# The pool of the weights placed behind the pools of the split inputs and the norm tiles

## The chip, the cores and the metric

The kernel runs on one core of one Trainium2 chip. The metric is the device time of one execution in microseconds (us); of several executions the median is given. A difference under about 0.2% of this kernel's time (2.5 us) can't be told from none.

## The reference

A decoder trunk of two layers over 512 tokens of width 1024, all in float32:

```
layer 0:  x = x + s5_mixer(rms_norm(x))       # state-space mixer, GELU, then z = y @ w_glu, gated
          x = x + conv_ffn(rms_norm(x))
          k, v = split(rms_norm(x) @ kv_w)    # shared keys and values
layer 1:  x = x + attention(rms_norm(x) @ w_q, k, v) @ w_o    # 16 heads of 64, stick-breaking, causal
          x = x + conv_ffn(rms_norm(x))
out = rms_norm(x)

conv_ffn(h):  g, u = split(h @ w_up)          # 2 x 2816 columns
              return (silu(conv3(g)) * u) @ w_down
```

## The kernel before

All activations lie transposed in SBUF: 128 channels on the partitions, 512 tokens along the free dimension, so that `x` is 8 tiles of 128x512. Each large product is float32 split in two: an operand is taken apart into a high part (`h`, rounded to float32r) and the rest (`l`), and the product is high x high + high x low + low x high. The helper `gemm` does this for one block of weights:

```
def gemm(bank, w, xs, k0=0, k1=KT, first=None, last=None):
    hi, lo = w
    for k in range(k0, min(k1, len(xs))):
        xh, xl = xs[k]
        c = slice(k * P, (k + 1) * P)
        mm(bank, hi[:, c], xh, ...)
        mm(bank, hi[:, c], xl, ...)
        mm(bank, lo[:, c], xh, ...)
```

In each `mm` (line 106) the second argument is loaded into TensorE as weights (a PEld row of the profile, 128x128, that is 512 bytes of each partition), and the third is streamed through (a PE row, 128x512, that is 2048 bytes of each partition). In these rows the weights' tile ends in `h` or `l` after the name of the matrix. The stages, with the tiles that meet in them (`out<-streamed, weights`; the profile prints the two operands in alphabetical order):

- State-space mixer, 0 to about 224 us. Its output product is `gl<-yh,wvh`, `gl<-yl,wvh`, `gl<-yh,wvl`.
- Feed-forward of layer 0, about 224 to 592 us, in three chunks of 8, 7 and 7 blocks of the 22 hidden blocks. Up-projections `fg` and `fu` stream the split input (`xh`, `xl`, or both halves of `xhl`) past `wgh`/`wgl` and `wuh`/`wul`; the down-projection `fd` streams the hidden activations `ah`, `al` past `wdh`/`wdl`.
- Attention, about 592 to 858 us. `kqb` (keys and queries) streams `xh`, `xl`, `xhl` past `awh`/`awl`; `v` (values) does it the other way round: the weights `awh`/`awl` are streamed, 256 columns at a time, and `xh`, `xl`, `xhl` are loaded. `z` and `ob<-wh,vv` are the attention's inner products, among tiles of the attention's own pools; `ob<-oh,awh` and its like are the output projection.
- Feed-forward of layer 1 with the final norm, about 858 us to the end. Its last block of `fd` is computed in two halves of 256 tokens.

Each weight block comes by DMA into a `raw` tile, ScalarE makes `hi` of it and VectorE `lo`. The order of the instructions is written out by hand in the mixer and in attention and left to the framework's scheduler elsewhere.

SBUF is given out by pools, which lie one behind the other in the order in which they are opened, and a tile keeps its place for the whole run. The ones concerned:

- `const`: parameters, `x`, constants.
- `wp`: 9 tiles of 4096 bytes per partition: three buffers each of `raw`, `hi` and `lo` (the mixer's first product and its rotation table use the same buffers).
- `tp`: 10 tiles of 2048 bytes (tag `ta`) and 3 of 4096 bytes (tag `tb`); `split_x` puts the split inputs `xh`, `xl`, `xhl` there, and the mixer its `u`, `u8`, `cm`.
- `sm`: 3 tiles of 2048 bytes for the norms and 18 tiny tiles of 32 bytes, 6720 bytes in all.
- the work pool of the current stage (`s5t`, `ff0`, `att`, `ff1`, and the pools nested in it): `yh`, `yl`, `ah`, `al`, `oh`, `ol`, `lh`, `wh`, `vv` and the rest.

All tiles of `wp`, `tp` and the work pools that TensorE's long products use are multiples of 512 bytes long, and the weights' slices are 512 bytes apart. So where an operand starts, counted modulo 512 bytes, depends on its pool alone.

Of the kernel before, what the change touches and what calls it, by code (L numbers as in the profile page):

```python
# [47 lines left out]
def trunk(ctx: ExitStack, tc: tile.TileContext, A, out):  # L48
# [1 line left out]
    V, SC, PE, GP = nc.vector, nc.scalar, nc.tensor, nc.gpsimd  # L50

    const = ctx.enter_context(tc.tile_pool(name="const", bufs=1))
    wp = ctx.enter_context(tc.tile_pool(name="wp", bufs=3))
    tp = ctx.enter_context(tc.tile_pool(name="tp", bufs=1))
    sm = ctx.enter_context(tc.tile_pool(name="sm", bufs=2))
    dr = ctx.enter_context(tc.tile_pool(name="dr", bufs=3, space=DRAM))

    cur = {}
# [1432 lines left out]
```

## Time and profile before

| | |
|---|---|
| median of 3 executions | 1237.41 us (1237.14 to 1238.03) |
| the profiled execution | 1236.96 us, of which the span from first to last instruction is 1235.2 us |
| granted TensorE clock | 0.997 |
| PE busy | 1207.6 us (98%), 6411 matrix products |
| DVE, ACT, POOL busy | 809.6, 539.3, 24.2 us |
| chain of waits that ended last | PE 89%, DVE 8% |

Times in the profile are counted from the span's start. PE is TensorE streaming, PEld its weight load, DVE is VectorE, ACT ScalarE, POOL GpSimd, SP the queue that issues most DMAs. The duration of a matrix product in a row holds the pipeline's depth as well; what a product costs in a dense row of them is the distance from one start to the next.

### The profile page before, as it was taken

What the parts mean: (1) busy time and instruction counts of PE and PEld (TensorE: products, weight loads), DVE (VectorE), ACT (ScalarE), POOL (GpSimd) and SP (SyncE); (2) the same over time, 40 slices, a digit from 0 to 9 for tenths busy, and PEclk for the clock granted to TensorE, in tenths of its full rate; (3) what the DMA queues carried; (4) which work ended last, traced back from release to release, by engine and by line L of the source; (5) the groups of instructions that cost most, each with busy time, mean ns of one, the idle gap of its engine ahead of it and who ended that gap; (6) DMA issues with size and microseconds to landing.
All of it is one profiled execution on the core that took longest, in us unless ns stands there. A gap on an engine that the chain in (4) does not pass through costs nothing.

```text
span 1235.2 us, 16227 instructions
## 1 busy us (share of the span) xinstructions
PE 1207.6 (98%) x6411; PEld 982.8 (80%) x6411; DVE 809.6 (66%) x1284; ACT 539.3 (44%) x866; POOL 24.2 (2%) x65
## 2 busy tenths in 40 slices
PE   7989999999999999999999999999999999999995
PEld 3457788788888888888889898888888888888884
DVE  7999764665435635557878989878655346536554
ACT  5234453433223323334577878765433233323331
POOL 1011020000000000000000000000000000000000
PEclk9999999999999999999999999999999999999998
DMA  5565443233233233233211211123233232332322
GB/s 199 150 166 140 122 124 98 86 102 98 90 102 99 82 106 101 92 91 100 76 51 53 82 55 48 39 86 103 86 102 97 91 103 86 91 113 88 94 75 69
DMA packets 55068, 118.47 MB, mean 96 GB/s; under 512 B 12912, under 2 KB 28528, under 8 KB 54992
## 3 DMA queue, kind: packets, MB, share of 16 engines
q1 hardware_dynamic: 50880, 105.55, 27.9%
q0 software_dynamic: 3248, 11.54, 3.1%
q8 instruction: 50, 0.82, 0.3%
q10 hardware_dynamic: 864, 0.35, 0.1%
q14 instruction: 26, 0.21, 0.1%
HBM read 109.03 MB, written 8.39 MB: 95 GB/s over the span
## 4 chain that ended last, share of the span: by engine, by line
PE 89%; DVE 8%; ACT 1%; issue 1%; DMA 1%; SPq 0%; DVEq 0%; ACTq 0%
PE fd L106 20%; PE fu L106 19%; PE fg L106 19%; PE kqb L106 7%; PE gl L106 6%; PE z L106 5%; PE ob L106 5%; PE v L106 4%; DVE k L112 2%; DVE p L112 1%; PE u L106 1%; PE y L106 1%; DVE cm L112 1%; DVE u L112 1%; DVE rv L670 1%
## 5 line engine op out<-in xcount | busy, mean ns | idle before, releaser
L106 PE MATMUL fd<-ah,wdh 128*128 128x512 f32 (+1 forms) x359 | 140.5, 391 | 0.0
L106 PE MATMUL fd<-ah,wdl 128*128 128x512 f32 (+1 forms) x359 | 139.2, 388 | 0.0
L106 PE MATMUL fd<-al,wdh 128*128 128x512 f32 (+1 forms) x359 | 137.9, 384 | 0.0
L112 DVE TENSOR_TENSOR x<-x,fd 128x512 f32<-128x512 f32 (+1 forms) x49 | 33.1, 676 | 119.8 <-PE fd L106 119.8
L157 ACT CAST wuh<-wur 128x1024 fp32r<-128x1024 f32 x44 | 46.4, 1054 | 134.4 <-PE fg L106 118.0
L157 ACT CAST wdh<-wdr 128x896 fp32r<-128x896 f32 (+1 forms) x48 | 47.1, 982 | 128.0 <-PE fd L106 98.2
L112 DVE TENSOR_TENSOR g<-fg,rb 128x512 f32<-128x512 f32 x44 | 30.4, 691 | 96.3 <-PE fg L106 93.5
L106 PE MATMUL fu<-xh,wuh 128*128 128x512 f32 x220 | 86.0, 391 | 0.0
L106 PE MATMUL fg<-xh,wgl 128*128 128x512 f32 x220 | 85.8, 390 | 0.0
L106 PE MATMUL fg<-xh,wgh 128*128 128x512 f32 x220 | 85.7, 390 | 0.0
L106 PE MATMUL fg<-xl,wgh 128*128 128x512 f32 x220 | 85.6, 389 | 0.0
L106 PE MATMUL fu<-xh,wul 128*128 128x512 f32 x220 | 85.6, 389 | 0.0
L106 PE MATMUL fu<-xl,wuh 128*128 128x512 f32 x220 | 85.6, 389 | 0.0
L112 DVE TENSOR_TENSOR u<-fu,rb 128x512 f32<-128x512 f32 x44 | 30.4, 691 | 80.5 <-PE fu L106 80.5
L106 PE MATMUL fu<-xhl,wuh 128*128 128x512 f32 x264 | 81.8, 391 | 0.0
L106 PE MATMUL fg<-xhl,wgh 128*128 128x512 f32 x264 | 81.5, 389 | 0.0
L106 PEld LDWEIGHTS fd<-ah,wdl 128*128 128x128 f32 x359 | 67.4, 188 | 15.2
L106 PEld LDWEIGHTS fd<-al,wdh 128*128 128x128 f32 x359 | 67.4, 188 | 14.8 <-issue 0.2
L106 PEld LDWEIGHTS fd<-ah,wdh 128*128 128x128 f32 x359 | 67.5, 188 | 13.2 <-issue 0.2
L157 ACT CAST wgh<-wgr 128x1024 fp32r<-128x1024 f32 x44 | 46.3, 1053 | 71.0 <-PE fd L106 33.0
L106 PE MATMUL u<-xg,wi 128*128 128x512 f32 x128 | 63.5, 628 | 7.5 <-ACT xg L270 7.5
L109 DVE SCALAR_TENSOR_TENSOR acc<-g,cw,acc 128x511 f32<-128x511 f32 x88 | 65.8, 747 | 2.4 <-ACT acc L832 0.9
(247 smaller groups left out, 2799.1 us busy)
## 6 DMA issues: line engine op xcount, KB each, us to landing
wgr<-in_w_up SPq DMA_DIRECT2D x44, 512.0 KB, 3.5
wur<-in_w_up SPq DMA_DIRECT2D x44, 512.0 KB, 3.5
wdr<-in_w_dn SPq DMA_DIRECT2D x32, 448.0 KB, 3.3
wdr<-in_w_dn SPq DMA_DIRECT2D x16, 512.0 KB, 3.5
wvr<-in_w_glu POOLq DMA_DIRECT2D x12, 512.0 KB, 3.8
ks<-kx SPq DMA_DIRECT2D x32, 128.0 KB, 2.5
m<-ks SPq DMA_DIRECT2D x8, 512.0 KB, 4.1
awr<-in_w_k SPq DMA_DIRECT2D x8, 512.0 KB, 3.5
```

Source lines behind the costliest of these rows:

```text
L106: PE.matmul(o, lhsT=lhsT, rhs=rhs, start=start, stop=stop, skip_group_check=True)
L109: (eng or V).scalar_tensor_tensor(out=o, in0=a, scalar=s, in1=b, op0=op0, op1=op1)
L112: (eng or V).tensor_tensor(out=o, in0=a, in1=b, op=op)
L157: SC.copy(out=hi, in_=raw)
L670: V.tensor_tensor_scan(out=rv[:, c], data0=decay[n], data1=wv[:, c], initial=0.0, op0=MUL, op1=ADD)
```

## The change

```
-    wp = ctx.enter_context(tc.tile_pool(name="wp", bufs=3))
     tp = ctx.enter_context(tc.tile_pool(name="tp", bufs=1))
     sm = ctx.enter_context(tc.tile_pool(name="sm", bufs=2))
+    wp = ctx.enter_context(tc.tile_pool(name="wp", bufs=3))
     dr = ctx.enter_context(tc.tile_pool(name="dr", bufs=3, space=DRAM))
```

Every engine has the same instructions in the same order with the same waits. Only the places in SBUF differ (bytes from the start of a partition, and the remainder modulo 512):

| pool | before | modulo 512 | after | modulo 512 |
|---|---|---|---|---|
| `wp` (36864 bytes) | 34976 | 160 | 74464 | 224 |
| `tp` (32768 bytes) | 71840 | 160 | 34976 | 160 |
| `sm` (6720 bytes) | 104608 | 160 | 67744 | 160 |
| work pools | 111328 | 224 | 111328 | 224 |

The 6720 bytes of `sm` are 13 times 512 and 64 more, which is why what lies behind `sm` starts at another remainder than what lies ahead of it.

More of the change, by code (lines that the diff above doesn't have):

```diff
@@ L52, in trunk @@
     const = ctx.enter_context(tc.tile_pool(name="const", bufs=1))
-    wp = ctx.enter_context(tc.tile_pool(name="wp", bufs=3))
     tp = ctx.enter_context(tc.tile_pool(name="tp", bufs=1))
     sm = ctx.enter_context(tc.tile_pool(name="sm", bufs=2))
+    wp = ctx.enter_context(tc.tile_pool(name="wp", bufs=3))
     dr = ctx.enter_context(tc.tile_pool(name="dr", bufs=3, space=DRAM))
```

## The prediction

> **What bounds the kernel now.** I read the totals and the chain of waits of the page first, then busy time by stage, then who waits for whom on TensorE.
>
> ```profile
> PE 1207.6 (98%) x6411; PEld 982.8 (80%) x6411; DVE 809.6 (66%) x1284; ACT 539.3 (44%) x866; POOL 24.2 (2%) x65
> PE 89%; DVE 8%; ACT 1%; issue 1%; DMA 1%; SPq 0%; DVEq 0%; ACTq 0%
> ```
> ```profile
> 0.00:157.00 157.00, 142.46 (x1340) 90.04 (x1341) 138.16 (x326) 66.09 (x151) 18.61 (x55) 1.00 0.53 153
> 157.00:224.00 67.00, 67.00 (x294) 54.77 (x293) 38.47 (x42) 27.47 (x36) 5.61 (x11) 1.00 0.38 116
> 224.00:614.00 390.00, 389.44 (x1763) 322.10 (x1762) 224.24 (x303) 140.30 (x178) 0.00 (x0) 1.00 0.31 95
> 614.00:858.00 244.00, 244.00 (x1400) 215.28 (x1400) 206.81 (x344) 183.69 (x355) 0.00 (x0) 1.00 0.20 61
> 858.00:1235.00 377.00, 364.65 (x1622) 300.59 (x1620) 201.93 (x271) 121.79 (x148) 0.00 (x0) 0.99 0.30 92
> ```
> ```profile
> PE stat L106 <- DVE acc L112: 0.5, 1, 0.5
> ```
>
> The windows' columns are PE, PEld, DVE, ACT and POOL busy (instructions), granted clock, DMA share, GB/s. From 157 us on TensorE is busy without a break; the last row is everything it waited for from 224 to 1220 us: 0.5 us. Nothing there can be won or lost by a DMA, by VectorE or by ScalarE as long as they keep this far ahead. Only the first 157 us hang on VectorE as well (138.16 busy). So the change acts on the time through one thing above all: how far apart TensorE's products follow each other. That is the view to read closely, and it shows something odd.
>
> ```profile
> L106 PE MATMUL fg<-xh,wgh x35: 389/389/390, 870.9 to 938.9; 128*128 128x512 f32 x35
> L106 PE MATMUL fd<-ah,wdh x59: 394/394/395, 949.8 to 989.6; 128*128 128x512 f32 x59
> L106 PE MATMUL fd<-al,wdh x59: 387/388/389, 950.0 to 989.8; 128*128 128x512 f32 x59
> L106 PE MATMUL fd<-ah,wdl x58: 392/392/393, 950.2 to 989.4; 128*128 128x512 f32 x58
> L106 PE MATMUL gl<-yh,wvh x91: 388/388/389, 162.1 to 223.9; 128*128 128x512 f32 x91
> L106 PE MATMUL ob<-oh,awh x34: 397/397/398, 834.2 to 857.3; 128*128 128x512 f32 x34
> ```
> ```profile
> 314.59 43.96 PE fd L106 x192
> 601.08 5.75 PE v L106 x48
> 826.88 31.26 PE ob L106 x137
> 947.18 43.96 PE fd L106 x192
> 1067.35 38.47 PE fd L106 x168
> ```
>
> Upper fence: one product's own rows (duration min/median/max, first and last start). Lower fence: stretches of the chain (start, length, count). From start to start:
> - `fg`, `fu`: between the first and the last of the 35 lie six rounds of 48 products (24 `fg`, 24 `fu`) and 12 more of the last `fg`: 300 in 68.0 us, 226.7 ns each.
> - `fd`: 192 in 43.96 us, 229.0 ns, twice over, and 168 in 38.47 us, 229.0. Within a group of three the durations are always 394, 388, 392.
> - `gl`: 90 groups of three in 61.8 us, 228.9 ns.
> - `ob` at the end of attention: 33 groups of three in 23.1 us, 233.3 ns.
>
> Same instruction, same shape, same clock, nothing waited for; and min, median and max differ by 2 ns, so this isn't disturbance by other engines. What differs is where the operands lie. `fg` streams from `tp` (160 modulo 512) past weights of `wp` (160): offset 0. `fd`, `gl` and `ob` stream from a work pool (224) past weights at 160: offset +64 bytes. I take it that TensorE's streaming and its load of the next weights meet in SBUF, and that the offset between the two, modulo some period, decides how often.
>
> That it is the offset and not the place of the streamed tile alone is shown by 256-column products. `v` (160 past 160) stands above, 48 in 5.75 us: 119.8 ns. The halved `fd` at the end (224 past 160) starts 20 products in 2.36 us, 118.0 ns:
>
> ```profile
> 1215.53 0.28 PE L106 MATMUL fd<-ah,wdh 128*128 128x256 f32 x1
> ...
> 1217.89 0.28 PE L106 MATMUL fd<-ah,wdl 128*128 128x256 f32 x1
> ```
>
> Here offset +64 is the better one, so 224 is no bad place in itself.
>
> **The change part by part.** Nothing is added, removed or reordered on any engine or queue. Three kinds of pairs change their offset.
>
> 1. `fd`, `gl`, `ob`: +64 becomes 0, the offset of `fg`. Price: 226.7 each.
>  - `fd`: 345 full-width products of each of three kinds, 1035 x (229.0 - 226.7) = 2.4 us less.
>  - `gl`: its last 300 or so lie in the PE-bound part, x 2.2 = 0.7 less; the rest lie beside VectorE's work before 157 us and count nothing.
>  - `ob`: 192; some 102 of them at 233.3, x 6.6 = 0.7, and 90 at about 229, x 2.3 = 0.2: 0.9 less.
> 2. `v` (streams weights past split inputs): 0 becomes +64. 384 products of 256 columns x (118.0 - 119.8) = 0.7 less. The 42 half-width `fd` go the other way: 0.1 more.
> 3. `fg`, `fu` and `kqb`: 0 becomes -64, which no row of before has. That is 44 x 48 = 2112 and 16 x 24 = 384 products, 2496 in all, two thirds of the long ones. Bounds: the best that an offset did is the 1.8 ns won at 256 columns, the worst the 6.6 ns of `ob`: from -4.5 to +16.5 us. I take 0.
>
> Why 0: the steps have a size. 256 more columns cost 226.7 - 119.8 = 106.9 ns, 0.418 per column; the 6.6 ns between `ob` and `fg` are 16 columns, 64 bytes. `fd` loses one such step in three products (3 x 2.3 = 6.9). And a row of products at offset 0 needs time to settle after other work:
>
> ```profile
> 740.21 0.40 PE L106 MATMUL kqb<-xl,awh 128*128 128x512 f32 x1
> ...
> 742.74 0.39 PE L106 MATMUL kqb<-xh,awh 128*128 128x512 f32 x1
> ...
> 745.23 0.39 PE L106 MATMUL kqb<-xh,awl 128*128 128x512 f32 x1
> ```
>
> The 11 products to 742.74 take 230 ns each, the 11 after it 226.4. So about 37 ns, five to six steps of 6.6, are lost before the row finds its place, then none. Two streams that repeat every 128 bytes would be in step after one lost step; five or six fit a period of 512 bytes, in which -64 and +64 are different cases. If slipping later mends every phase at offset 0, and +64 is just over the edge (one step in three), then -64 lies on the other side of offset 0, away from that edge. That is a guess from few rows, and its chance is put accordingly.
>
> The Trainium skill (TensorE: Matmul & The Clock Gate, "Step-by-step: what each phase is for") says that TensorE has two independent SBUF read ports, so that loading the next weights takes no bandwidth from the running product. By that rule the pools' order would not matter at all; the trace's 226.7 against 229.0 and 233.3 disagrees unless something else than the offset makes them.
>
> Other engines: `hi` and `lo` are made from `raw` inside `wp`, so their mutual offsets stay; the mixer's rotation table meets other tiles from `wp` in ten steps before 157 us. No row prices that; DVE's 138 us of work there would have to change by 2% to show. DMAs land in `raw` at another place with the same length.
>
> Sum: -2.4 - 0.7 - 0.9 - 0.7 + 0.1 = -4.6 us, plus 2496 x 0. Against the profiled execution's 1236.96 us that is 1232.4; the median stands 0.45 above that execution, so 1232.8.
>
> **The rivals.**
> - *-64 costs what +64 costs* (2.3 ns): 2496 x 2.3 = 5.7 more, sum +1.1, 1238.5 us: no change. For it: symmetry, and a period of 128 bytes, in which they are the same offset. Against: the five to six steps above.
> - *-64 settles like `ob`, one step in every product*: 16.5 more, sum +11.9, 1249.3 us, slower by 1%. It decides alone from 2.8 ns per product on, since 2496 x 2.8 covers the 4.6 won and 2.5 more. For it: the same offset +64 is seen in two states, 229.0 and 233.3. Against: of some 1600 long products at +64 only the 100 or so of late `ob` stayed in the bad one.
> - *-64 is better than 0*, as +64 is at 256 columns: up to 4.5 less, 1228.3 us. Against: at 512 columns no steady row is under 226.7.
> - *The offset doesn't matter* and the work pool's tiles are slow for a reason that stays: 1237.4 us, the median of before. Against: the 256-column rows. The Trainium skill's rule of two read ports (above) would give this too.
>
> **How the numbers follow.** Chances: 0.40 for my sum, 0.27 for the mirror image, 0.18 for a dear -64 (half or all of the products in the bad state), 0.09 for a better -64, 0.06 for no effect. The range reaches from 1227.5 (a better -64) to 1241 (past the mirror image's 1238.5, with a few products in the bad state); it leaves out nearly all of the dear case. The likeliest case's own range is 1231 to 1234.5. Faster by over 0.2% (2.5 us, which a measurement can tell): my sum and the better case, 0.48. Slower: the dear case and a little of the mirror image, 0.22. The rest, 0.30, is the same.
>
> **What would show it.** Right: the chain's `fd` x192 in 43.5 us instead of 43.96, with durations 389 throughout; `gl` and late `ob` at 226.7; `v` x48 at 5.66. The disputed term is read from `fg<-xh,wgh` x35 between its first and last start: 68.0 us if -64 costs nothing, 68.7 in the mirror image, 70.0 if dear. The prediction is wrong if `fg` and `fu` lose more than 1 ns each, or if `fd` stays at 229.0.

## The result, and the profile after

The changed kernel takes 1247.4 us at the median (1246.99 to 1248.08) against 1237.04 us (1236.81 to 1238.03): ratio 1.0081, 95% interval 1.0071 to 1.0092. It is slower by 10 us, where 4.6 us less was forecast; the case that came true is the second rival, a dear -64. The profiled execution took 1247.35 us, its span 1245.5.

The totals, the share of the chain of waits, and everything TensorE waited for from 224 to 1230 us, show the same machine as before, PE-bound, with no new wait:

```profile
PE 1217.5 (98%) x6411; PEld 981.2 (79%) x6411; DVE 809.2 (65%) x1284; ACT 539.8 (43%) x866; POOL 24.3 (2%) x65
PE 89%; DVE 8%; DMA 1%; ACT 1%; issue 1%; SPq 0%; DVEq 0%; ACTq 0%
```
```profile
PE stat L106 <- DVE acc L112: 0.3, 1, 0.3
```

PE is busy for 9.9 us more, the span is 10.3 longer, and the other engines' sums are what they were (DVE 809.6, now 809.2). So the products themselves follow each other more slowly. The same products as in the prediction (duration min/median/max, first and last start):

```profile
L106 PE MATMUL fg<-xh,wgh x35: 393/393/398, 875.7 to 945.7; 128*128 128x512 f32 x35
L106 PE MATMUL fd<-ah,wdh x64: 389/389/398, 954.1 to 997.0; 128*128 128x512 f32 x64
L106 PE MATMUL fd<-al,wdh x64: 389/389/395, 954.4 to 997.2; 128*128 128x512 f32 x64
L106 PE MATMUL fd<-ah,wdl x64: 389/389/393, 954.6 to 997.4; 128*128 128x512 f32 x64
L106 PE MATMUL gl<-yh,wvh x92: 389/389/389, 161.9 to 223.8; 128*128 128x512 f32 x92
L106 PE MATMUL ob<-oh,awh x35: 389/389/389, 837.6 to 862.0; 128*128 128x512 f32 x35
```

`fg` needs 70.0 us for its 300 products, 233.3 ns each: the value that the prediction named for a dear -64. `fd` has the flat 389 that `fg` had. `gl` starts 273 products (three for each of 91 steps) in 61.9 us, 226.7 ns each, and late `ob` has 389 where it had 397.

The chain of waits, as far as it answers to the stretches shown of before (start, length, count), with one more row of before behind it:

```profile
155.46 68.97 PE gl L106 x303
316.72 43.54 PE fd L106 x192
438.66 38.10 PE fd L106 x168
606.48 5.65 PE v L106 x48
689.38 5.60 PE kqb L106 x24
832.34 30.54 PE ob L106 x137
954.28 43.54 PE fd L106 x192
```
```profile
434.76 38.47 PE fd L106 x168
```

`fd` x192 fell from 43.96 to 43.54, `v` x48 from 5.75 to 5.65, `ob` x137 from 31.26 to 30.54, `gl` from 69.57 to 68.97. What lies between two stretches of `fd` is a chunk's up-projection: from 314.59 + 43.96 to 434.76 us it took 76.2 us before; from 316.72 + 43.54 to 438.66 it takes 78.4. Added up over the run, by the first starts of each stage in the two traces: six up-projections +13.4 us, six down-projections -2.3, attention -0.6, mixer -0.1; together +10.4 us, which is the longer span (10.3 from the rounded spans). `gl` won 0.60 us, but in the changed kernel its stretch begins 0.49 later, so the mixer's end gains almost nothing; why its first part ends later isn't known.

### The profile page after: what moved, and what is told of

It is laid out like the page before. It is cut to its first block, busy times and chain, and to the rows that moved or that the text cites. A ratio compares the mean times of both kernels' runs of the same rounds, so it can differ in the third digit from the quotient of the medians.

```text
span 1245.5 us, 16227 instructions
## 1 busy us (share of the span) xinstructions
PE 1217.5 (98%) x6411; PEld 981.2 (79%) x6411; DVE 809.2 (65%) x1284; ACT 539.8 (43%) x866; POOL 24.3 (2%) x65
## 4 chain that ended last, share of the span: by engine, by line
PE 89%; DVE 8%; DMA 1%; ACT 1%; issue 1%; SPq 0%; DVEq 0%; ACTq 0%
PE fu L106 20%; PE fg L106 19%; PE fd L106 19%; PE kqb L106 7%; PE gl L106 6%; PE z L106 5%; PE ob L106 5%; PE v L106 4%; DVE k L112 2%; DVE p L112 1%; PE u L106 1%; PE y L106 1%; DVE cm L112 1%; DVE u L112 1%; DVE rv L670 1%
## 5 line engine op out<-in xcount | busy, mean ns | idle before, releaser
L106 PEld LDWEIGHTS fd<-ah,wdh 128*128 128x128 f32 x359 | 67.4, 188 | 13.9 <-issue 0.2
L106 PEld LDWEIGHTS fd<-ah,wdl 128*128 128x128 f32 x359 | 67.4, 188 | 13.4
```

The costliest lines, as they stand in the source:

```text
L106: PE.matmul(o, lhsT=lhsT, rhs=rhs, start=start, stop=stop, skip_group_check=True)
```

## The experiments

Theory: the spacing of TensorE's long products is set by the offset between the streamed tile and the weights, modulo some number of bytes. Rivals: it is the place itself (how far back the weights lie, which pools are neighbours), or each tile's own remainder. The runs move pools alone; the instructions stay, but for the last one's mixer.

**All offsets 0, in either order (e1_all0, e2_all0_behind).** The tiny tiles of `rstd` get a pool of their own, `ti`, ahead of everything:

```
+    ti = ctx.enter_context(tc.tile_pool(name="ti", bufs=2))   # e1: ti, wp, tp, sm
     ...                                                       # e2: ti, tp, sm, wp
-        v = sm.tile([P, 4], F32, name="sv")                   # and six like it
+        v = ti.tile([P, 4], F32, name="sv")
```

e1_all0:

> The 18 tiny tiles (576 bytes) lie in a pool of their own ahead of the weights' pool, in the order of before, so that weights, split inputs and work pools all start at 224 modulo 512: every long product has offset 0. Theory offset (the offset of streamed tile and weights modulo 512 sets the spacing): fg, fu, fd, gl, late ob all at 226.7 ns, v of 256 columns at 119.8; the time is 3.9 us under before, 1233.2 us (ratio 0.9968). Rival place (weights that start at 224 modulo 512, or that lie farther back, are loaded later in each product): fg and fu at 233.3 as in the changed kernel, time near 1247 us.

e2_all0_behind:

> The same with the order of the changed kernel: tiny tiles first, then split inputs, norms, weights, work pools; all start at 224 modulo 512 and the weights' pool lies at the very same bytes as in the changed kernel. Theory offset: as the run before, 1233.2 us, fg at 226.7. Rival place: the weights haven't moved against the changed kernel, so fg and fu stay at 233.3, time near 1247 us.

Measured: 1232.92 us, ratio to before 0.9962 (0.995 to 0.9975), and 1233.68 us, 0.9964 (0.9951 to 0.9976). First e1, then e2:

```profile
L106 PE MATMUL fg<-xh,wgh x35: 389/389/389, 868.1 to 936.1; 128*128 128x512 f32 x35
```
```profile
944.41 43.52 PE fd L106 x192
```
```profile
L106 PE MATMUL fg<-xh,wgh x35: 389/389/389, 868.8 to 936.8; 128*128 128x512 f32 x35
```

`fg` needs 68.0 us again, 226.7 ns each, and now `fd` does too. In e2 the weights lie at the very bytes where they lie in the changed kernel; only the split inputs (by 576 bytes), the norms and the tiny tiles moved, and the whole loss is gone. So it isn't the place of the weights. Both kernels beat before and after; the 0.8 us between the two can't be told from none.

**Same offsets, other places (e3_place).** Pools in the order `tp`, `ti`, `wp`, `sm`:

> Split inputs, tiny tiles, weights, norms, work pools: the weights lie directly behind the split inputs and 6 KB nearer to them than in the changed kernel, with the same remainders (160, 224, 224). Theory offset: same as the changed kernel, 1247.4 us, fg 233.3, fd 226.7. Rival distance (how far apart the pools lie, or that weights and work pool are neighbours, decides): the norms now lie between weights and work pool, so fd or fg move, by at least 1 ns.

Measured: 1247.11 us, ratio 1.0074 (1.006 to 1.0087), as the changed kernel. A stretch of `fg` in layer 0:

```profile
L106 PE MATMUL fg<-xh,wgh x35: 394/394/394, 360.5 to 430.5; 128*128 128x512 f32 x35
```

70.0 us for 300, 233.3 ns. That weights and work pool are no longer neighbours does nothing.

**Everything 32 bytes further on (e4_shift32).** An empty tile of 32 bytes per partition ahead of `wp`:

> Before, with 32 bytes left free ahead of the weights' pool: all pools move by 32 bytes (192, 192, 256 modulo 512), every offset stays. Theory offset: same as before, 1237.0 us, fg 226.7, fd 229.0. Rival own remainder (a tile that doesn't start on a line of 64 bytes costs a line): all tiles now start at a multiple of 64, so fg falls below 226.7 and the time by several us.

Measured: 1238.0 us, ratio 1.0002 (0.9992 to 1.0011): no difference, and the rows are those of before (`fg` 68.0 us, `fd` x192 43.96):

```profile
L106 PE MATMUL fg<-xh,wgh x35: 389/389/389, 872.0 to 940.0; 128*128 128x512 f32 x35
```
```profile
315.37 43.96 PE fd L106 x192
```

So a tile's own remainder doesn't count, as far as a step of 32 bytes shows; the offset between the two does.

**Other offsets (p64, p128, p256, p32, m128).** One execution each, at a granted clock of 0.995 to 0.997; what is read is the spacing within the trace. An empty tile stands between `wp` and `tp` (p64 and its like), or between `tp` and `wp` in the order `tp`, `wp`, `sm` (m128):

```
     wp = ...
+    ctx.enter_context(tc.tile_pool(name="pad", bufs=1)).tile([P, 16], F32, name="pad")   # 64 bytes
     tp = ...
```

p64:

> Before, with 64 bytes left free between the weights' pool and the pool of the split inputs: fg, fu and kqb get offset +64, fd, gl and ob get +128, v gets -64. Theory offset: fg at 229.0 like fd of before (the offset counts, whichever product it is). Rival role (the up-projection at any offset but 0 costs a full step): fg at 233.3. fd at +128 is not known: 229 to 233 if every offset but 0 costs, 226.7 if only the neighbours of 0 do.

p128:

> 128 bytes free there: fg +128, fd, gl, ob +192, v -128. Period 512: fg at +128 repeats what fd shows at +128 in the run with 64 bytes. Period 128 or 256 (rival): fg at +128 is 226.7 (128) or what -128 gives (256).

p256:

> 256 bytes free there: fg and v at 256 (half a period), fd, gl, ob at -192. Period 512: fg differs from offset 0. Period 256 or 128 (rival): fg back at 226.7 and fd at 229.0 as in before.

m128:

> Split inputs, 128 free bytes, weights, norms, work pools: fg, fu, kqb at -128, fd, gl, ob at +64, v at +128. Theory offset: fd at 229.0 as in before, though the weights start at 288 and the work pools at 352 modulo 512. fg at -128: 233.3 if the dear side of 0 goes on, less if -64 was its worst point.

p32:

> Before, with 32 bytes left free between the weights' pool and the pool of the split inputs: fg, fu and kqb at +32, fd, gl and ob at +96, v at -32. Theory lines of 64 bytes: fg at +32 is like 0 or like +64 (226.7 or 229.0), fd at +96 like +64 or +128 (229.0 or 232.5). Rival smooth: values between them, 227.8 and 230.7.

Measured: 1246.93, 1255.21, 1237.23, 1250.23 and 1257.78 us, beside 1237.6 to 1237.7 of before. Each fence is one kernel, in the order p64, p128, p256, m128, p32; the row of `fg` spans 300 products (of layer 1 in p64 and p256, of the second chunk of layer 0 in the others), `fd` is 192. The fence of m128 has two rows more, from its first chunk and from late `ob`:

```profile
L106 PE MATMUL fg<-xh,wgh x35: 388/388/389, 877.0 to 945.6; 128*128 128x512 f32 x35
318.49 44.61 PE fd L106 x192
```
```profile
L106 PE MATMUL fg<-xh,wgh x35: 390/393/404, 362.8 to 432.5; 128*128 128x512 f32 x35
318.17 44.79 PE fd L106 x192
```
```profile
L106 PE MATMUL fg<-xh,wgh x35: 389/389/390, 871.1 to 939.1; 128*128 128x512 f32 x35
314.77 43.96 PE fd L106 x192
```
```profile
L106 PE MATMUL fg<-xh,wgh x35: 390/393/404, 361.4 to 431.1; 128*128 128x512 f32 x35
317.64 43.94 PE fd L106 x192
239.24 5.60 PE fg L106 x24
834.14 31.26 PE ob L106 x137
```
```profile
L106 PE MATMUL fg<-xh,wgh x35: 392/396/397, 363.8 to 433.8; 128*128 128x512 f32 x35
319.16 44.79 PE fd L106 x192
```

Divided out, and put together with before and after (offset of the streamed tile against the weights, modulo 256; ns per product of 512 columns):

| offset | ns | seen in |
|---|---|---|
| 0 | 226.7 | `fg` of before, e1, e2; `fd` of after; `fg` of p256 (256 bytes) |
| 32 | 233.3 | `fg` of p32 |
| 64 | 229.0 | `fd` of before; `fd` of p256 (-192); 228.9 in `fd` of m128, 228.7 in `fg` of p64 |
| 64 | 233.3 | late `ob` of before, e4, p256 and m128 |
| 96 | 233.3 | `fd` of p32 |
| 128 | 232.3 | `fd` of p64; `fg` of p128 and of m128 (-128), second chunk |
| 128 | 233.3 | `fg` of p128 and of m128, first chunk (24 in 5.60 us) |
| 192 | 233.3 | `fg` of after (-64), of e3; `fd` of p128 |

Period 256 fits every row: 256 bytes apart is like 0, -192 like +64, -128 like +128. And -64 is +192. The expectation for p256 named a period of 512, and there it missed: `fg` and `fd` came out as in before. The role of the product is not what sets the price: `fg` at +64 has `fd`'s price (p64), which speaks against the rival that it names. The expectation for p128 that `fg` there repeats `fd` of p64 held (69.7 us for 300 and 44.61 for 192, 232.3 both). At +32 neither expectation held: neither a value of a neighbour nor one between them, but the highest.

The offset alone does not fix the price, however. At 64 and at 128 two steady spacings occur, the second always 233.3. It isn't chance: late `ob` takes the same 31.26 us for 137 in all four kernels that have it at 64. Nor is it the product: in before, `ob` runs at 228.8 ns up to 832.7 us, and after a few short products of `vv` at 233.3. That points to what ran just before a row, but no run tests it.

**Which load does a streamed tile meet? (n64).** The low parts of the weights, and those of the first five split inputs, in pools of their own 64 bytes further on:

```
+    wl, tl = (ctx.enter_context(tc.tile_pool(name=n, bufs=1)) for n in ("wl", "tl"))   # behind sm
-        lo = wp.tile([P, 8 * P], F32R, tag="lo", name=name + "l")[:, :cols * P]
+        lo = wl.tile([P, 8 * P], F32R, tag="lo", name=name + "l", bufs=3)[:, :cols * P]
-            h, l = T("xh", F32R, "ta"), T("xl", F32R, "ta")
+            h, l = T("xh", F32R, "ta"), T("xl", F32R, "tl")
...
```

> The low parts of the weights and the low parts of the first five split inputs lie in pools of their own 64 bytes further on (224 modulo 512; high parts, and both parts of inputs 5 to 7, stay at 160). Read in fg and fu, inputs 0 to 4: against its own weights a streamed tile has offset 0, +64, -64 in the three products; against the weights that are loaded while it streams, those of the next product, it has 0, 0, 0. Theory next load (streaming meets the load of the next weights): 226.7 ns each there. Rival own weights: (226.7 + 229.0 + 233.3) / 3 = 229.7. Inputs 5 to 7 have one product in three at -64 in either theory, some 2.2 more on the mean. The mixer's first part is scheduled slightly differently, so the total is not compared.

Measured (the total was 1248.91 us):

```profile
L106 PE MATMUL fg<-xh,wgh x35: 389/395/395, 362.3 to 431.8; 128*128 128x512 f32 x35
```

69.5 us for 300, 231.7 ns over all inputs; by start to start, inputs 0 to 4 alone have 231.4 on the mean. The theory of the next load gave 226.7 for them, the rival 229.7. Neither came out, and inputs 5 to 7, expected some 2.2 above the others, have 231.7. A sum over pairs, each with its own steady price, doesn't describe it. But this doesn't refute either theory: only 15 products in a row keep the pattern before the 9 of inputs 5 to 7 break it, and the row of `kqb` in the prediction needed 11 to settle at offset 0. Which load it is stays open.

## Why the prediction was wrong

- *What bounds the kernel, and what the change acts on*: right. Nothing but the spacing of TensorE's products moved, and the offset sets it (e2, e3, e4).
- *Step 1* (+64 becomes 0): right. `fd` was to come to 43.5 us per 192 and came to 43.54; 2.4 us less were forecast for it, 2.3 measured. `gl` and `ob` went to the flat 389. The 0.7 us of `gl` showed in its own stretch (0.60) and hardly in the time, since it began 0.49 later.
- *Step 2* (`v` from 0 to +64): right in sign; 5.66 us forecast for 48 that took 5.75, and 5.65 measured.
- *Step 3* (0 becomes -64) failed. I took 0 for a price that the bounds put between -1.8 and +6.6 ns; it is the upper bound, 6.6 ns, 233.3 against 226.7. For `fg` and `fu` that is 13.4 us, and with the other stages' -3.0 the whole result.
- The step inside it that failed is the reading of the settling row. I read five to six lost steps as a sign of a period of 512 bytes, in which -64 and +64 are different cases, and then placed -64 "on the other side, away from that edge". The period is 256 (p256), and -64 is +192, as dear as any offset tried. Nor are there two sides: of the offsets tried only 0 runs at 226.7, +64 comes close, and 32, 96, 128 and 192 cost 232.3 to 233.3. The number of lost steps was no measure of the period. That 233.3 is the price of a row that hasn't settled, and that at -64 a row never does, would fit: 64 and 128 are seen both with it and below it, 32, 96 and 192 only with it. No run shows that this is how it works.
- `kqb` cost 1.3 us more (added up from start to start over attention in both traces), not the 2.5 that 384 x 6.6 gives. Before the change its rows of 24 were not at 226.7 throughout: x24 took 5.49 at 684 us, 228.8 each, and takes 5.60 now. That, 13.4 us instead of 13.9 for `fg` and `fu`, and a median of before that was 0.4 lower than the prediction's are why 1247.4 came out below the rival's 1249.3, although `gl` gave less than forecast.
- That the offset counts and not the place was called shown by the 256-column rows; they compare two different products, so there it was only argued. It is e2, e3 and e4 that show it. Why the chip behaves so, the meeting of two streams in SBUF, no run shows.
- The Trainium skill's rule of two read ports (TensorE: Matmul & The Clock Gate, "Step-by-step: what each phase is for") would have given no change. The trace disagrees: with the same instructions the spacing of `fg` goes from 226.7 to 233.3 ns when only the operands' offset changes.

## What to carry to other kernels

In a PE-bound row of products where each loads new weights, read the distance from start to start, not only busy time: where two rows of equal shape and clock differ by a few ns, always by the same, look at where their operands start. For products of 512 columns, start all tiles that meet in TensorE at the same remainder modulo 256 bytes; a handful of tiny tiles in a pool between them is enough to break it, and putting those tiny tiles ahead of the large pools took this kernel from 1237.6 to 1232.9 us. And where the price of a case lies between bounds far apart, with the worse end already seen in the trace as a steady state, a guess at the mechanism from one short row is no reason to take the better end.

## What the runs showed of the hardware

- For float32r products of 512 columns with new weights each time, the spacing is 226.7 ns at offset 0 modulo 256 bytes (before, e1, e2), 229.0 at 64 (before; late `ob` 233.3), 232.3 or 233.3 at 128 (p128, m128), and 233.3 at 32, 96 and 192 (p32, after).
- At 256 columns the order is another. Stretches of 24 `v` take 2.93 us at offset 0 (before), 2.87 at 64 (after) and 2.81 at 192 (p64), which is 122, 120 and 117 ns each; over all 384 `v` the means are 120.8, 118.5 and 117.5.
- Moving both operands by 32 bytes (e4) or the weights by 38912 and the split inputs by 36864 bytes with the offset kept at 0 (e2 against e1) changes nothing that can be measured.
